# Hybrid decoder layer on one core: two products between gate sums and their splits, another load and split order ahead of the last projection, one weight sum moved

## Chip, core, metric

The kernel runs on one core of a Trainium2 chip. The metric is device time in microseconds of one execution. Engines: PE (TensorE, matmuls), DVE (VectorE), ACT (ScalarE), POOL (GpSimd), SP (SyncE, which issues nearly all transfers). Each engine works through its own instructions in order.

## The reference

One layer over 1024 tokens of width 1024, all in float32, cut to what matters here:

```python
proj = rmsnorm(x, norm_g) @ w_in                       # 9 kinds of columns
o_gla = gla_chunked(g_q, g_k, g_v, log_a)              # 4 heads, state carried over chunks
o_gla = rmsnorm(o_gla, gla_norm_g) * silu(g_gate)
y_a = o_gla @ w_pa
o_sb = stick_breaking(s_q, s_k, s_v) * silu(s_gate)    # 8 heads, causal, 128-query blocks
y_b = o_sb @ w_pb
gates = sigmoid(m_logits + b_gate)
x = x + (gates[0] * y_a + gates[1] * y_b) @ w_o
return rmsnorm(x, final_g)
```

## The kernel before

Every float32 operand is split into two float32r parts: ACT copies it to a high part, DVE subtracts that from the source for the low part (`split`, lines 167 to 169, and `o_hi`/`o_lo`, 1444 and 1448). A product then takes three matmuls per block of 128: high by high, high by low, low by high. The big projections use a Winograd form of a 2x2 block product: seven products of half-size operands instead of eight, on sums such as S1 to S4 (of the activations) and T1 to T4 (of the weights). A "product" below is 12 matmuls of 128x512.

- **Projection of w_in.** `pair_job` makes 31 jobs of seven products each, `Pairs` hands them out by units: `pairs.run(n)` does n products. In each job POOL makes T1 to T4 from the raw weights (lines 247 to 250), ACT and DVE split them. The first 25 products run beside the decay's exponentials (`djobs`), and beside `pjobs`: blocks j = 0 to 3 of w_pa are loaded, four sums each are made on DVE (`tp_sum`, 831), and the result is stored to `d_tp`, through one buffer. The next products up to `GLA_AT` = 63 run beside `tjobs`: the same for eight blocks of w_pb and w_o, into `d_t`.
- **GLA.** 32 steps (head h, block b of 128 tokens), with four products of the projection between the parts of each step. `gl_out` makes the block's output on PE and its norm: ACT sums squares, DVE scales, POOL takes the power (234), DVE multiplies (997). One step later `gl_gate` transposes it, multiplies it by the gate tile g (1007), splits and stores it. For b of 4 and more it then goes on at once: POOL makes four sums of g and of the gate tile gp four blocks back (1020), ACT and DVE split them, SP stores them to `d_os`. They are operands of the product with w_pa later. Tile g has four buffers, loaded by `gl_g`. ACT, DVE, PE, POOL and SP follow here the order that the tile scheduler gives them.
- **Stick-breaking attention.** 8 heads by 8 blocks: scores, sigmoid, a running product on DVE (1123), transposes and values; `values` multiplies by the gate (1161) and stores to `d_osb` (1163). Between them `Line` puts the products with w_pa (`pa_a`, `pa_b`, `pa_c`), listed by hand.
- **Transition.** The last eight products with w_pa, `pa_d`: for i = 0 to 3 first S3 by T3 (J = 1), then A22 by T4 into the same bank (J = 0). After each, `out_put` adds (1275), multiplies with the gate (1276) and stores. PE may go on in a bank only when DVE's addition has read it. Beside them the operands of the last projection (w_pb) are loaded from `d_osb` (A11, A12, A21, A22 by `a_load`, four 256 KB pieces each) and from w_pb and `d_t` (B11, B21, T2 and others by `o_load`), split, and summed on POOL (`sums`, 1406). From `manual.enter_context` on, the order on ACT, DVE and PE is the order of the code: all four splits of A11, two products, the splits of B11, two products, and so on.
- **Last projections.** 28 products with w_pb (`a_product`, four to each u), where `a_keep` and `a_merge` (the addition "kept", 1538) free the banks, then 28 with w_o, and the final norm.

## Time and profile before

| | |
|---|---|
| median of three runs | 1208.29 us (1207.48 to 1208.4) |
| the profiled execution | 1205.1 us |
| its span, first to last instruction | 1203.1 us |
| granted PE clock over the span | 0.992 |
| moved by DMA | 274.92 MB, 229 GB/s in the mean |

The span in 40 equal slices of 30 us, busy share in tenths, and the granted clock:

```profile
PE   8999999999999999999999999999999996899997
PEld 8998877887888788778888877888888885688886
DVE  6797776888677786776775776457888795978986
ACT  6556652333455555544444444235546353355543
POOL 1022221424243342542452252000000000900001
PEclk9999999999999999999999999999999997999999
```

Slices 0 to 9 are the projection up to GLA, 10 to 23 GLA, 24 and 25 the rest of the projection, 26 to 32 the attention, 33 and 34 the transition, the rest the last projections. A row of the timeline gives start, length, engine, line, operation, the tiles out<-in with their shape, and in brackets how long the engine had been idle before it and what ended the wait.

### The profile page before, as it was taken

How to read it: one execution, taken by the hardware profiler on the slowest of the kernel's cores; microseconds unless marked ns; L12 is line 12 of the kernel's file. 1: busy time of each engine (PE TensorE's matmuls, PEld its weight loads, DVE VectorE, ACT ScalarE, POOL GpSimd, SP SyncE). 2: the span in 40 equal slices, each digit the busy share in tenths (PEclk: the TensorE clock that was granted, in tenths of full speed). 3: DMA queues.
4: the chain of work that ended last, by engine and by line, in shares of the span. 5: the costliest groups of instructions: out<-in, count | busy, mean ns of one | idle time of the engine just before them, and what ended most of it. 6: DMA issues, size and time to landing. Idle time of an engine off the chain costs nothing.

```text
span 1203.1 us, 17066 instructions
## 1 busy us (share of the span) xinstructions
PE 1158.9 (96%) x5775; PEld 972.1 (81%) x5775; DVE 915.6 (76%) x1519; ACT 576.0 (48%) x1088; POOL 282.2 (23%) x281
## 2 busy tenths in 40 slices
PE   8999999999999999999999999999999996899997
PEld 8998877887888788778888877888888885688886
DVE  6797776888677786776775776457888795978986
ACT  6556652333455555544444444235546353355543
POOL 1022221424243342542452252000000000900001
PEclk9999999999999999999999999999999997999999
DMA  7326869997456765764655467889868879748652
GB/s 283 124 62 201 308 225 344 312 328 271 146 187 206 241 216 183 243 208 132 214 154 162 153 200 244 284 285 310 297 211 312 290 252 321 274 152 285 222 193 105
DMA packets 229299, 274.92 MB, mean 229 GB/s; under 512 B 14390, under 2 KB 165068, under 8 KB 226140
## 3 DMA queue, kind: packets, MB, share of 16 engines
q1 hardware_dynamic: 228636, 272.86, 68.6%
q8 instruction: 45, 0.74, 0.2%
q10 hardware_dynamic: 576, 0.98, 0.2%
q14 instruction: 42, 0.34, 0.1%
HBM read 168.93 MB, written 104.86 MB: 228 GB/s over the span
## 4 chain that ended last, share of the span: by engine, by line
PE 72%; issue 6%; DMA 6%; POOL 6%; DVE 6%; ACT 2%; SPq 1%; POOLq 0%; DVEq 0%; ACTq 0%
PE pp L273 12%; PE pp L274 12%; PE pp L275 12%; POOL g L1020 2%; PE pp L226 2%; PE pp L1254 1%; PE pp L1255 1%; PE pp L1256 1%; PE av L1156 1%; PE av L1158 1%; PE av L1157 1%; PE xa L1502 1%; PE xa L1501 1%; PE xa L1503 1%; PE xb L1625 1%
## 5 line engine op out<-in xcount | busy, mean ns | idle before, releaser
L273 PE MATMUL pp<-S,wh 128*128 128x512 f32 x372 | 147.4, 396 | 1.5 <-DVE f L555 1.5
L274 PE MATMUL pp<-S,wh 128*128 128x512 f32 x372 | 145.0, 390 | 0.0
L275 PE MATMUL pp<-S,wl 128*128 128x512 f32 x372 | 145.0, 390 | 0.0
L247 POOL TENSOR_TENSOR tt<-raw 128x512 f32<-128x512 f32 x31 | 43.4, 1400 | 267.9 <-DVE wl L169 256.4
L169 DVE TENSOR_TENSOR wl<-tt,wh 128x1024 fp32r<-128x1024 f32 x62 | 76.9, 1240 | 35.1 <-ACT wh L168 34.6
L312 DVE TENSOR_TENSOR f<-pp,f 128x512 f32<-128x512 f32 x93 | 63.7, 686 | 51.1 <-PE pp L275 46.4
L168 ACT ACTIVATE wh<-tt 128x1024 fp32r<-128x1024 f32 x62 | 65.6, 1057 | 63.0 <-PE pp L274 54.5
L1123 DVE TENSOR_TENSOR_SCAN be<-be,m 128x128 f32<-128x128 f32 (+3 forms) x64 | 86.2, 1349 | 4.9 <-ACT be L1120 4.9
L168 ACT ACTIVATE wh<-raw 128x1024 fp32r<-128x1024 f32 (+1 forms) x52 | 53.6, 1031 | 73.4 <-PE pp L274 31.3
L279 ACT ACTIVATE f<-pp 128x512 f32<-128x512 f32 x93 | 54.7, 590 | 65.2 <-PE pp L275 61.6
L169 DVE TENSOR_TENSOR wl<-raw,wh 128x1024 fp32r<-128x1024 f32 (+1 forms) x52 | 71.3, 1372 | 18.0 <-ACT wh L168 15.9
L273 PEld LDWEIGHTS pp<-S,wh 128*128 128x128 f32 x372 | 70.6, 190 | 16.6 <-ACT wh L168 1.9
L275 PEld LDWEIGHTS pp<-S,wl 128*128 128x128 f32 x372 | 69.9, 188 | 14.9
L274 PEld LDWEIGHTS pp<-S,wh 128*128 128x128 f32 x372 | 70.0, 188 | 13.7
L1120 ACT ACTIVATE be<-z 128x384 f32<-128x384 f32 (+4 forms) x96 | 47.0, 493 | 41.6 <-PE z L1119 35.6
L1406 POOL TENSOR_TENSOR N<-A,A 128x512 f32<-128x512 f32 x4 | 7.1, 1784 | 244.9 <-DMA A<-d_osb 244.9
L273 PE MATMUL pp<-ha22h,wh 128*128 128x512 f32 x124 | 49.4, 399 | 4.9 <-DVE f L312 4.9
L273 PE MATMUL pp<-S,dh 128*128 128x512 f32 x124 | 48.9, 394 | 3.7 <-ACT f L279 3.7
L234 POOL TENSOR_TENSOR r<-r,nhalf 128x1 f32<-128x1 f32 x40 | 24.0, 600 | 115.7 <-DVE r L233 114.4
L1020 POOL TENSOR_TENSOR g<-g 128x128 f32<-128x128 f32 x64 | 34.1, 532 | 71.4 <-DVE o L169 64.1
L273 PE MATMUL pp<-ha11h,wh 128*128 128x512 f32 x124 | 49.2, 397 | 0.0
L273 PE MATMUL pp<-ha12h,wh 128*128 128x512 f32 x124 | 49.0, 395 | 0.0
(556 smaller groups left out, 3504.1 us busy)
## 6 DMA issues: line engine op xcount, KB each, us to landing
raw<-in_w_in_dram SPq DMA_DIRECT2D x31, 1024.0 KB, 6.5
d_t<-t SPq DMA_DIRECT2D x16, 512.0 KB, 5.2
d_ogl<-o SPq DMA_DIRECT2D x64, 128.0 KB, 2.3
d_q<-o SPq DMA_DIRECT2D x16, 512.0 KB, 3.5
d_k<-o SPq DMA_DIRECT2D x16, 512.0 KB, 4.6
d_os<-o SPq DMA_DIRECT2D x32, 256.0 KB, 2.6
d_v<-o SPq DMA_DIRECT2D x32, 256.0 KB, 3.3
k<-d_k SPq DMA_DIRECT2D x8, 1024.0 KB, 6.1
```

The lines of the kernel that those rows point to most:

```text
L168: nc.scalar.activation(hi, src, AF.Copy)
L169: eng.tensor_sub(lo, src, hi.bitcast(F32))
L226: nc.tensor.matmul(pt[:, 0:n], *ops[kb][i], start=k == 0, stop=k == 3 * KB - 1)
L247: nc.gpsimd.tensor_sub(t1, b[:, 0, 1], b[:, 0, 0])
L273: nc.tensor.matmul(pt, bh[:, j], ah[:, j], start=first and j == 0, stop=False, skip_group_check=True)
L274: nc.tensor.matmul(pt, bh[:, j], al[:, j], start=False, stop=False, skip_group_check=True)
L275: nc.tensor.matmul(pt, bl[:, j], ah[:, j], start=False, stop=j == 3, skip_group_check=True)
L279: nc.scalar.activation(t[nm], t[bank], AF.Copy)
L312: nc.vector.tensor_add(add, bank, add)
L1020: nc.gpsimd.tensor_tensor(dst, x1, x2_, op=fn)
L1120: nc.scalar.activation(om[:, off + pc * w:off + (pc + 1) * w], zt[:, 0:w], AF.Sigmoid, scale=-inv_sqrt)
L1123: nc.vector.tensor_tensor_scan(rest, rest, m1[:, off:T][:, ::-1], 1.0, op0=ALU.mult, op1=ALU.max)
```

## The change

It has four parts, in the diff below.

1. GLA: the sums and their splits leave `gl_gate`. `gl_sum` (POOL) comes at the end of the step, `gl_sums_out` (splits and store) after two more products, ahead of `gl_g`; its place in ACT's and DVE's order is held.
2. The fourth block of w_pa (j = 3) moves from `pjobs` to `tjobs` as k = 8, the third block's later sums go from product 17 to 20, and `GLA_AT` is 67, so that GLA starts four products later.
3. Transition, loads: A11 ahead of the last weights (`wlast`), B21, the fourth pieces of A21 and A22 and T2 only after the last A load (`issue_after`), and pool `pq` on the other side. `pd_load(2)` moves into the attention's line, with two tiles of its own.
4. Transition, order of ACT and DVE: the splits of A11, B11 and A12 in halves between the additions of `pa_d`, which is called for one i at a time.

```diff
-GLA_AT = 63
+GLA_AT = 67
-    for j, (load_at, *sums_at, store_at) in enumerate(((0, 3, 4, 5), (6, 8, 10, 11), (12, 15, 17, 18), (19, 22, 23, 24))):
+    for j, (load_at, *sums_at, store_at) in enumerate(((0, 3, 4, 5), (6, 8, 10, 11), (12, 15, 20, 21))):
...
-    for k in range(8):
+    for k in range(9):
...
     def gl_gate(h, b):
-        t = gblk.pop((h, b))
+        t = gblk[h, b]
...
+    def gl_sum(h, b):
+        if b < 4:
             return
-        g, gp = t["g"], t["gp"]
+        g, gp = (gblk[h, b][nm] for nm in ("g", "gp"))
...
             nc.gpsimd.tensor_tensor(dst, x1, x2_, op=fn)
+    def gl_sums_out(h, b):
+        t = gblk.pop((h, b))
+        if b < 4:
+            return
         o = stage().rearrange("p e (s c) -> p e s c", c=P)
-        for i, src in enumerate((g, gp)):
-            split(src, *(o[:, e, 2 * i:2 * i + 2] for e in range(2)))
+        for i, nm in enumerate(("g", "gp")):
+            hi, lo = (o[:, e, 2 * i:2 * i + 2] for e in range(2))
+            tc.keep_in_program_order(nc.scalar.activation(hi, t[nm], AF.Copy))
+            tc.keep_in_program_order(nc.vector.tensor_sub(lo, t[nm], hi.bitcast(F32)))
...
         pairs.run(2)
+        if s > 1:
+            gl_sums_out(*steps[s - 2])
         gl_g(h, b)
         pairs.run(2)
         if s:
             gl_gate(*steps[s - 1])
         gl_out(h, b)
+        if s:
+            gl_sum(*steps[s - 1])
     pairs.run(3)
+    gl_sums_out(*steps[-2])
     gl_gate(*steps[-1])
+    gl_sum(*steps[-1])
+    pairs.run(2)
+    gl_sums_out(*steps[-1])
...
-    o_split("bA11", ALL)
-    st.run(1)
-    o_split("bB11", AB)
-    o_load("bB21")
-    a_load("A21", [3])
-    a_load("A22", [3])
+    o_split("bA11", (0, 1))
+    pa_d(0, 1)
+    o_split("bA11", (2, 3))
+    pa_d(1, 1)
+    wq_split("T4", 1, wlast)
+    pa_d(0, 0)
+    pd_load(3, (1,))[0]()
+    o_split("bB11", AB[:1])
+    pa_d(1, 0)
+    pd_load(3, (0,))[0]()
+    with tc.issue_after(last_a):
+        o_load("bB21")
+        a_load("A21", [3])
+        a_load("A22", [3])
+        o_load("bT2", "tt")
     sums("b", range(3), ("S1", "S3", "S2"), nc.gpsimd)
-    o_load("bT2", "tt")
+    pa_d(2, 1)
+    o_split("bB11", AB[1:])
```

SP's order at the transition before, from the last product's gate loads (`o<-d_ga`) to A11: `raw_10380` is B21, `tt_10401` T2, `d_osb7` the last store of the attention.

```order
L1306 DMA o_10367<-d_ga5_144 128x512
L1308 DMA o_10367<-d_ga4_143 128x512
L1422 DMA raw_10380<-in_w_pb_dram 128x4x128 x3
L1416 DMA tt_10401<-d_t0_165 128x512
L1416 DMA tt_10401<-d_t1_166 128x512
L1224 DMA wlast_10282<-d_tp_173 128x4x256
L1163 DMA d_osb7_115<-f_10237 128x512
L1396 DMA A11_10284<-d_osb0_108 128x512
L1396 DMA A11_10286<-d_osb2_110 128x512
L1396 DMA A11_10288<-d_osb4_112 128x512
L1396 DMA A11_10290<-d_osb6_114 128x512
```

And after the change, at the same place:

```order
L1333 DMA o_10211<-d_ga5_144 128x512
L1333 DMA o_10211<-d_ga4_143 128x512
L1413 DMA A11_10290<-d_osb0_108 128x512
L1413 DMA A11_10292<-d_osb2_110 128x512
L1185 DMA d_osb7_115<-f_10245 128x512
L1413 DMA A11_10294<-d_osb4_112 128x512
L1413 DMA A11_10296<-d_osb6_114 128x512
L1246 DMA wlast_10303<-d_tp_173 128x4x256
L1413 DMA A12_10305<-d_osb1_109 128x512
```

Two pieces of A11 now stand ahead of the attention's last store, the other two right behind it, and B21 and T2 follow the A loads further down.

DVE's order at the transition before, from the attention's last values (L1161) to the fourth pair of addition and multiplication of `pa_d`:

```order
L1161 SCALAR_TENSOR_TENSOR f_10237<-av_10239,vend_231,f_10237 128x128 x4
L1448 TENSOR_TENSOR bA11l_10320<-A11_10284,bA11h_10319 128x512
L1448 TENSOR_TENSOR bA11l_10320<-A11_10286,bA11h_10319 128x512
L1448 TENSOR_TENSOR bA11l_10320<-A11_10288,bA11h_10319 128x512
L1448 TENSOR_TENSOR bA11l_10320<-A11_10290,bA11h_10319 128x512
L1275 TENSOR_TENSOR f_10197<-pp_10329,f_10197 128x512
L1276 TENSOR_TENSOR f_10197<-f_10197,o_10196 128x512
L1275 TENSOR_TENSOR f_10204<-pp_10346,f_10204 128x512
L1276 TENSOR_TENSOR f_10204<-f_10204,o_10203 128x512
L169 TENSOR_TENSOR wl_10364<-wlast_10282,wh_10363 128x1024
L1448 TENSOR_TENSOR bB11l_10375<-raw_10292,bB11h_10374 128x1024 x2
L1275 TENSOR_TENSOR f_10198<-pp_10329,f_10198 128x512
```

And after it, from the same place:

```order
L1183 SCALAR_TENSOR_TENSOR f_10245<-av_10247,vend_231,f_10245 128x128 x4
L1466 TENSOR_TENSOR bA11l_10328<-A11_10290,bA11h_10327 128x512
L1466 TENSOR_TENSOR bA11l_10328<-A11_10292,bA11h_10327 128x512
L1297 TENSOR_TENSOR f_10198<-pp_10333,f_10198 128x512
L1298 TENSOR_TENSOR f_10198<-f_10198,o_10197 128x512
L1466 TENSOR_TENSOR bA11l_10328<-A11_10294,bA11h_10327 128x512
L1466 TENSOR_TENSOR bA11l_10328<-A11_10296,bA11h_10327 128x512
L1297 TENSOR_TENSOR f_10205<-pp_10354,f_10205 128x512
L1298 TENSOR_TENSOR f_10205<-f_10205,o_10204 128x512
L169 TENSOR_TENSOR wl_10372<-wlast_10303,wh_10371 128x1024
L1297 TENSOR_TENSOR f_10201<-pp_10333,f_10201 128x512
```

The first addition stands behind two splits instead of four, the second behind the other two, and the third no longer behind those of B11.

ACT's order in GLA before, in the step of head 0, block 6 (`o` from `g` are the splits of gate and sums, `wh` and `f` belong to the projection, `f` frees a bank):

```order
L168 ACTIVATE o_3966<-g_3766 128x256
L994 ACTIVATE on_3989,ssq_3990<-po_3982 128x256
L168 ACTIVATE knh_4019<-tr_4017 128x128
L168 ACTIVATE ash_4003<-am1_2693 128x128
L168 ACTIVATE o_3975<-g_3766 128x256
L168 ACTIVATE o_3975<-g_3768 128x256
L168 ACTIVATE wh_4038<-tt_3647 128x1024
L279 ACTIVATE f_4036<-pp_4023 128x512
```

And after it, for the same block (L1036 are the splits of the sums):

```order
L168 ACTIVATE o_4040<-g_3844 128x256
L168 ACTIVATE vh_4074<-vr_3928 128x256
L168 ACTIVATE knh_4086<-tr_4084 128x128
L168 ACTIVATE qsh_4232<-q2_3637 128x128
L168 ACTIVATE ash_4070<-am1_2771 128x128
L279 ACTIVATE f_4107<-pp_4094 128x512
L168 ACTIVATE wh_4143<-raw_3848 128x1024
L168 ACTIVATE o_4130<-f_4107 128x512
L1036 ACTIVATE o_4134<-g_3844 128x256
L1036 ACTIVATE o_4134<-g_3846 128x256
```

Before, the sums' splits follow the gate's within four instructions and stand ahead of `wh` and `f`; after, `f` and a weight split come between.

## The prediction

> **What bounds the kernel now.** I read the page's busy shares first, then its clock row and its chain, then every wait of TensorE (PE) in order of time, and for each long wait the other engines in the same microseconds.

> ```profile
> span 1203.1 us, 17066 instructions
> PE 1158.9 (96%) x5775; PEld 972.1 (81%) x5775; DVE 915.6 (76%) x1519; ACT 576.0 (48%) x1088; POOL 282.2 (23%) x281
> ...
> PE 72%; issue 6%; DMA 6%; POOL 6%; DVE 6%; ACT 2%; SPq 1%; POOLq 0%; DVEq 0%; ACTq 0%
> ```

> PE is busy for 96% and carries 72% of the chain, so an edit that leaves the matmuls alone can win only PE's idle time and slowed clock: 1203.1 - 1158.9 = 44.2 us, less what stays at both ends. The stretches say where it lies:

> ```profile
> 400.00:730.00 330.00, 321.53 (x1598) 262.85 (x1597) 242.66 (x524) 158.50 (x356) 126.29 (x139) 1.00 0.62 191
> 990.00:1045.00 55.00, 39.67 (x168) 31.96 (x167) 40.13 (x48) 19.32 (x29) 23.06 (x13) 0.84 0.83 285
> ```

> The columns are the stretch, its length, PE, PEld, DVE, ACT and POOL busy, the granted clock, DMA share and GB/s. In 990 to 1045 (last attention block, last four products with w_pa, first operands of the last projection) PE idles 15.3 us and the clock is 0.84; in 400 to 730 (GLA) it idles 8.5 us at full clock. These are the PE rows of the first place:

> ```profile
> 1006.70 0.39 PE L1256 MATMUL pp<-oa22h,wl 128*128 128x512 f32 x1
> 1018.16 0.79 PE L1254 MATMUL pp<-oa21h,wh 128*128 128x512 f32 x1 [11.08 <-DVE f L1275]
> 1022.87 0.40 PE L1256 MATMUL pp<-oa21h,wl 128*128 128x512 f32 x1
> 1035.71 0.47 PE L1254 MATMUL pp<-oa21h,wh 128*128 128x512 f32 x1 [4.25 <-DVE f L1275]
> 1040.13 0.39 PE L1254 MATMUL pp<-oa21h,wh 128*128 128x512 f32 x1
> 1061.89 0.39 PE L1501 MATMUL pp<-bA12h,bB21h 128*128 128x512 f32 x1
> 1062.12 0.39 PE L1502 MATMUL pp<-bA12l,bB21h 128*128 128x512 f32 x1
> ```

> At full clock matmuls of this shape start 0.23 us apart (the last two rows), so a product of 12 takes 2.75 us. From 1018.16 to 1022.87 eleven starts take 4.7 us instead of 2.5, from 1035.71 to 1040.13 twelve take 4.4 instead of 2.8. The two waits with their slow clock cost 11.1 + 2.2 + 4.25 + 1.6 = **19.2 us**. Both wait for the Vector (DVE) addition L1275, which frees the bank. Why that addition is late:

> ```profile
> 1005.06 1.13 DVE L1161 SCALAR_TENSOR_TENSOR f<-av,vend,f 128x128 f32<-128x128 f32 x4 [5.17 <-PE av L1158]
> 1014.87 2.64 DVE L1448 TENSOR_TENSOR bA11l<-A,bA11h 128x512 fp32r<-128x512 f32 x4 [8.68 <-ACT bA11h L1444]
> 1017.42 0.68 DVE L1275 TENSOR_TENSOR f<-pp,f 128x512 f32<-128x512 f32 x1
> 1014.20 2.58 ACT L1444 ACTIVATE bA11h<-A 128x512 fp32r<-128x512 f32 x4 [16.46 <-DMA A<-d_osb]
> 1001.78 0.33 SPq L1306 DMA_DIRECT2D o<-d_ga  x1
> 1002.62 2.13 SPq L1422 DMA_DIRECT2D raw<-in_w_pb_dram  x3
> 1006.56 0.56 SPq L1163 DMA_DIRECT2D d_osb<-f  x1
> 1007.16 10.66 SPq L1396 DMA_DIRECT2D A<-d_osb  x14
> ```

> The addition's own data lie ready; it stands behind four splits of A11, whose loads leave SP only from 1007.16.

> **The change, transition.** SP now puts A11's first two loads where the three raw loads began (1002.62), ahead of the store of 1006.56; its other two follow that store, and B21 and T2 come after all A loads. How long a 256 KB transfer takes here is bounded by two rows, and a load of that size just ahead lies between them:

> ```profile
> A<-d_osb SPq DMA_DIRECT2D x16, 256.0 KB, 5.4
> o<-d_ga SPq DMA_DIRECT2D x4, 256.0 KB, 4.1
> d_w<-f SPq DMA_DIRECT2D x1, 256.0 KB, 3.3
> ```

> I take 4.1, the nearest row (2.1 us of issue time for other loads is gone from ahead of it, but the line isn't empty). A11's second piece: issued 1003.1, landed 1007.2, ACT 0.65 (2.58/4), DVE 0.66 (2.64/4), the addition 0.68: PE resumes at 1009.2 and has waited 2.3 us since 1006.9. It then does one product to 1012.0. Its next bank needs the second addition, now behind pieces three and four: issued by 1007.7, landed 1011.8, through by 1013.8; a second wait of 1.8 us. Afterwards each addition stands in DVE's row before PE needs its bank: six products of 2.75 us are fed one by one, and the wait of 4.25 us, made by four splits ahead of the third pair of additions, is gone. PE then starts the last projection at 1027.5 and is at its eighth product, the one at 1061.89 now, by 1046.8.

> There DVE is late next. Its rows of now, with the GpSimd (POOL) sums beside them:

> ```profile
> 1021.78 1.95 POOL L1406 TENSOR_TENSOR N<-A,A 128x512 f32<-128x512 f32 x1 [244.95 <-DMA A<-d_osb]
> 1028.15 6.82 DVE L1448 TENSOR_TENSOR bA12l<-A,bA12h 128x512 fp32r<-128x512 f32 x4
> 1051.82 2.35 DVE L1448 TENSOR_TENSOR bT2l<-tt,bT2h 128x1024 fp32r<-128x1024 f32 x2
> 1056.65 0.69 DVE L1538 TENSOR_TENSOR kept<-pp,kept 128x512 f32<-128x512 f32 x1 [2.49 <-PE pp L1503]
> ```

> From 1014.87 to the end of bT2l at 1054.2 DVE has 39.3 us of work without a pause, and all of it still comes before the first addition "kept", which frees the bank of the eighth product. Now it may begin at 1006.2, when L1161 is done; it stands still 1.2 us for A11's first piece and 2.0 us for its third, and ends at 1006.2 + 39.3 + 3.2 = 1048.7; with the addition 1049.4. So PE reaches the eighth product at 1049.4 instead of 1061.9: **12.5 us** won, not 19.2. Bounds: with 3.3 us landings and no pause of DVE 15.7 (1046.2); with 5.4 us landings (2.6 us more over the two waits, at the price of a slowed clock of 1.6 if one of them passes 4 us) about 8. Behind that point the splits of S1, T1, S3 and T3 take DVE no longer than their products take PE, so I let the gain stand to the end.

> The Vector splits slow down beside POOL: four bA12l take 6.82 us, four bA11l alone 2.64. [...] The sum goes by the rows.

> **The change, GLA.** PE's waits in the GLA stretch, and what stands behind them:

> ```profile
> 409.29 0.50 PE L273 MATMUL pp<-S,dh 128*128 128x512 f32 x1 [2.19 <-ACT f L279]
> 500.35 0.50 PE L273 MATMUL pp<-S,dh 128*128 128x512 f32 x1 [1.49 <-ACT f L279]
> 527.32 0.50 PE L273 MATMUL pp<-ha22h,wh 128*128 128x512 f32 x1 [1.70 <-DVE f L312]
> 716.94 0.44 PE L1004 MATMUL tr<-ident,on 128*128 128x128 f32 x2 [0.94 <-DVE o L169]
> 725.51 0.63 PE L615 MATMUL tr<-ident,f 128*128 128x128 f32 x4 [1.48 <-DVE f L610]
> ...
> 407.39 0.42 ACT L168 ACTIVATE o<-g 128x256 fp32r<-128x256 f32 x1 [1.13 <-POOL g L1020]
> 407.71 1.04 ACT L168 ACTIVATE wh<-tt 128x1024 fp32r<-128x1024 f32 x1
> ...
> ACT o L168 <- POOL g L1020: 40.8, 29, 3.7
> ...
> L1020 POOL TENSOR_TENSOR g<-g 128x128 f32<-128x128 f32 x64 | 34.1, 532 | 71.4 <-DVE o L169 64.1
> ```

> Read backwards from 409.29: PE waits for ScalarE's (ACT) copy f, which came after the split wh at 407.71, which came after the split of the gate sum at 407.39, which waited for POOL. The other rows end in the same way. The five waits are 7.8 us. The change puts two products (5.5 us) and more between POOL's four sums (0.53 us each, with a power between them) and their splits, so these no longer stand still, and the copies of the projection no longer queue behind a POOL chain. What is late next is the power of the norm on POOL and the weight splits, both as before; and a start four products later shifts the partners. I leave one wait of 1.3 us: **6.5 us** won. Bounds: 7.8, and 3.0 if two waits like the largest now and one like 0.94 come at new places. The g loads now wait for sums two steps old; they are asked for one and a half steps (16 us) before use, and SP, on which they stand, has that much time.

> **The moved weight sum.**

> ```profile
> 161.99 0.50 PE L273 MATMUL pp<-ha22h,wh 128*128 128x512 f32 x1 [1.72 <-DVE f L312]
> 158.81 1.39 DVE L831 TENSOR_TENSOR tp<-tp 128x512 f32<-128x512 f32 x2
> 170.77 0.99 DVE L803 COPY ebl<-e 128x16 f32<-128x16 f32 x1 [2.92 <-ACT e L799]
> 190.98 0.47 PE L273 MATMUL pp<-S,wh 128*128 128x512 f32 x1 [1.50 <-DVE f L555]
> ```

> Two tp sums leave DVE at 158.81 and take **1.4 us** out of the wait at 161.99; three products later DVE idles (2.92 before 170.77) and hides them. The fourth block's four loads, four sums and store leave this stretch for one 30 products later. That may free the DMA line and end the wait at 190.98, or cost as much at the new place: between -1.5 and +1.5, and I take 0.

> **Sum.** 12.5 + 6.5 + 1.4 = 20.4 us. The profiled execution took 1205.1 us (span 1203.1, 2.0 around it), so it would take 1184.7; the three runs shown have a median of 1208.29, 3.2 above it, and there it is 1187.9: **1188 us**.

> **Rivals.**
> - *Vector binds the transition.* POOL's sums start some 5 us earlier and meet more of DVE's list, or the first loads take 5.4 us. For it: DVE has no pause in those 39.3 us now. Against it: POOL's work is no more than before. Gain 8 to 4 instead of 12.5, about 1195. [...]
> - *The GLA waits move instead of going.* All ACT and DVE rows there have other partners after a shift of four products. Gain 0 instead of 6.5: 1194. Against it: five of five waits end at POOL's gate sums.
> - *It doesn't do what it says.* A11 lands no sooner, since the DMA line and not SP's order set 1014.20: then the 19.2 stay and only 7.9 are won, 1200. Against it: four raw loads, two loads of T2 and the last weights leave the line ahead of it.
> - *Slower.* In GLA's 16 steps with sums, SP stands at the load of g until the splits two steps later have read the old tile, and weight loads queue behind it. It decides from a hold of 16 us, the lead of those loads; past it, each step would lose about what its waits are now, up to 2.2 us, and the price would be 35 us against 20.4: 1223.

> **Numbers.** Forecast 0.62, Vector 0.16, moved waits 0.11, no effect on the loads 0.05, slower 0.03, a cancelling mixture within 0.2% 0.03. The range takes in the bounds: best 15.7 + 7.8 + 2.9 = 26.4, 1182; worst 8 + 3 - 0.1 = 11, 1197. With a margin for the first two rivals it is 1181 to 1199, which leaves out the last three cases (0.11). About 0.2% (2.4 us) is what a measurement of this kernel can tell from no change. Faster 0.93, same 0.03, slower 0.04.

> **What would show it.** Right: PE's wait near 1006 is 1.5 to 3 us at full clock, a second of about 2 follows, one of 1 to 3 us stands at the eighth product of the projection, behind "kept"; ACT has nearly no wait for POOL's g, and the rows at 409, 500, 527, 717 and 725 are gone. Wrong: ACT's first bA11h starts after 1009 (counted from the same PE end), the clock in that stretch stays below 0.95, or PE waits of over 1 us appear in GLA behind other releasers.

## The result and the profile after

The median of five runs is 1188.7 us (1188.39 to 1191.52), beside 1208.29 us for the kernel before in the same series: a ratio of 0.9848, with a 95% interval of 0.9829 to 0.9866. The runs fall into two groups, three near 1188.5 us with a mean granted clock of 0.995 to 0.997, two at 1191.2 and 1191.5 with 0.993 and 0.994. The profiled one is the longest. The profile before lies 3.2 us below its median, this one 2.8 above: the spans differ by 13.6 us where the medians differ by 19.6.

From the page of the changed kernel, the span, the busy time and the granted clock (40 slices):

```profile
span 1189.5 us, 17064 instructions
...
PE 1160.4 (98%) x5775; PEld 972.5 (82%) x5775; DVE 916.9 (77%) x1519; ACT 577.1 (49%) x1088; POOL 278.3 (23%) x281
...
PEclk9999999999999999999999999999999999989999
```

PE is busy as long as before (1160.4 against 1158.9 us) in a shorter span: its pauses went, not its work. The two stretches of the prediction, same columns:

```profile
400.00:730.00 330.00, 327.61 (x1628) 268.60 (x1627) 246.58 (x540) 161.16 (x364) 124.01 (x143) 1.00 0.61 190
990.00:1045.00 55.00, 47.71 (x202) 38.34 (x202) 43.28 (x46) 22.68 (x34) 28.17 (x16) 0.95 0.87 295
```

In GLA PE idles 2.4 us instead of 8.5. ACT's waits for POOL's gate sums, 40.8 us in 29 waits before, are now (sum, number, longest):

```profile
ACT o L1036 <- POOL g L1026: 9.0, 6, 4.2
```

In 990 to 1045, which now reaches into the last projection, 7.3 instead of 15.3. PE's longest waits around GLA and in the transition, in order of time, with the matmuls behind them:

```profile
296.53 0.50 PE L273 MATMUL pp<-ha22h,wh 128*128 128x512 f32 x1 [2.30 <-DVE f L312]
429.72 0.50 PE L273 MATMUL pp<-ha22h,wh 128*128 128x512 f32 x1 [1.13 <-DVE f L312]
1001.29 0.50 PE L1276 MATMUL pp<-oa21h,wh 128*128 128x512 f32 x1 [2.30 <-DVE f L1297]
1002.38 0.63 PE L1276 MATMUL pp<-oa21h,wh 128*128 128x512 f32 x1
1002.81 0.63 PE L1277 MATMUL pp<-oa21l,wh 128*128 128x512 f32 x1
1043.93 0.80 PE L1531 MATMUL pp<-bA12h,bB21h 128*128 128x512 f32 x1 [4.99 <-DVE kept L1568]
1044.53 0.63 PE L1532 MATMUL pp<-bA12l,bB21h 128*128 128x512 f32 x1
1049.22 0.54 PE L1531 MATMUL xa<-bS2h,bT2h 128*128 128x512 f32 x1
```

The first wait of the transition is the 2.30 us that was forecast, but matmuls behind it start 0.43 us apart. The second transition wait of the prediction didn't come. The wait behind "kept" came with 4.99 us instead of some 2.6 (1049.4 - 1046.8), and the product behind it took 5.3 us (1043.93 to 1049.22) instead of 2.75.

What stood ahead of these waits on the other engines:

```profile
994.32 0.90 SPq L1413 DMA_DIRECT2D A<-d_osb  x2
998.67 1.19 ACT L1462 ACTIVATE bA11h<-A 128x512 fp32r<-128x512 f32 x2 [9.02 <-DMA A<-d_osb]
999.34 1.29 DVE L1466 TENSOR_TENSOR bA11l<-A,bA11h 128x512 fp32r<-128x512 f32 x2 [1.25 <-ACT bA11h L1462]
1002.76 1.30 DVE L1466 TENSOR_TENSOR bA11l<-A,bA11h 128x512 fp32r<-128x512 f32 x2 [0.73 <-ACT bA11h L1462]
1006.78 1.23 DVE L169 TENSOR_TENSOR wl<-wlast,wh 128x1024 fp32r<-128x1024 f32 x1 [1.33 <-ACT wh L168]
1027.21 6.19 POOL L1424 TENSOR_TENSOR A<-A,A 128x512 f32<-128x512 f32 x3
1038.53 0.63 ACT L1462 ACTIVATE bS2h<-A 128x512 fp32r<-128x512 f32 x1 [10.61 <-POOL A L1424]
1039.19 1.21 DVE L1466 TENSOR_TENSOR bS2l<-A,bS2h 128x512 fp32r<-128x512 f32 x1 [1.84 <-ACT bS2h L1462]
1043.19 0.68 DVE L1568 TENSOR_TENSOR kept<-pp,kept 128x512 f32<-128x512 f32 x1
```

A11's first loads now leave at 994.3 and are there for ACT at 998.7. Towards the end ACT stands 10.61 us for POOL: POOL made three S4 sums (6.19 us) before the sums of the fourth piece, whose S2 is needed first.

The ratio is that of all runs of a kernel to the kernel before in the same series (the medians of before lie between 1205.5 and 1208.3 us), and gains in us below are worked out from it. The stages are read from each kernel's one profile, by starts in the trace: the front (up to the last scores of the attention), from there to the first product S2 by T2 (transition and eight products), from there to the first product of w_o's T4. The rest is 18.4 to 18.8 us in all. PE's idle time in GLA is given where it is used; for the changed kernel it starts behind the wait at 296.53.

| kernel | ratio to before, 95% interval | front | scores to S2·T2 | S2·T2 to T4 | idle in GLA |
|---|---|---|---|---|---|
| before | 1 | 986.6 | 78.0 | 119.7 | 8.7 |
| changed | 0.9848 (0.9829 to 0.9866) | 978.5 | 70.7 | 121.7 | 3.2 |
| part 1 alone | 0.9917 (0.9901 to 0.9932) | 981.0 | 77.7 | 119.7 | 1.2 |
| part 2 alone | 1.0006 (0.9996 to 1.0016) | 989.9 | 79.0 | 119.7 | 11.0 |
| parts 3, 4 | 0.9944 (0.9932 to 0.9956) | 988.0 | 71.4 | 121.5 | 8.6 |
| part 3 alone | 0.9981 (0.9970 to 0.9992) | 988.7 | 73.9 | 121.5 | |
| part 4 alone | 0.9961 (0.9946 to 0.9976) | 987.3 | 71.7 | 120.2 | |
| parts 1, 3, 4 | 0.9868 (0.9851 to 0.9885) | 977.3 | 71.1 | 122.0 | |
| parts 1, 2, 4 | 0.9879 (0.9863 to 0.9896) | 977.6 | 72.3 | 121.3 | |
| changed, POOL's order | 0.9851 (0.9832 to 0.9869) | 975.2 | 69.6 | 121.9 | 2.5 |
| and T2 behind kept | 0.9835 (0.9819 to 0.9852) | 977.4 | 65.2 | 122.6 | |
| changed, 672 bytes | 0.9850 (0.9833 to 0.9866) | 979.1 | 69.5 | 119.7 | |
| all three | 0.9822 (0.9808 to 0.9837) | 978.1 | 65.4 | 120.9 | |

One thousandth is 1.2 us.

### The profile page after: what moved, and what is told of

The parts are those of the page before. It is cut to its first block, busy times and chain, and to the rows that moved or that the text cites. A ratio compares the mean times of both kernels' runs of the same rounds, so it can differ in the third digit from the quotient of the medians.

```text
span 1189.5 us, 17064 instructions
## 1 busy us (share of the span) xinstructions
PE 1160.4 (98%) x5775; PEld 972.5 (82%) x5775; DVE 916.9 (77%) x1519; ACT 577.1 (49%) x1088; POOL 278.3 (23%) x281
## 3 DMA queue, kind: packets, MB, share of 16 engines
q1 hardware_dynamic: 228780, 272.86, 69.6%
## 4 chain that ended last, share of the span: by engine, by line
PE 53%; DVE 5%; issue 2%; DMA 2%; SPq 1%; ACT 1%; POOL 1%; POOLq 0%; DVEq 0%; ACTq 0%
PE pp L273 8%; PE pp L274 8%; PE pp L275 8%; PE av L1178 1%; PE av L1180 1%; PE av L1179 1%; PE pp L1277 1%; PE pp L1278 1%; PE pp L1276 1%; PE tr L1157 1%; PE xb L1656 1%; PE xb L1655 1%; PE xb L1657 1%; PE z L1139 1%; PE z L1141 1%
## 5 line engine op out<-in xcount | busy, mean ns | idle before, releaser
L273 PE MATMUL pp<-S,wh 128*128 128x512 f32 x372 | 147.1, 395 | 0.0
L169 DVE TENSOR_TENSOR wl<-tt,wh 128x1024 fp32r<-128x1024 f32 x62 | 76.8, 1239 | 34.3 <-ACT wh L168 34.1
L312 DVE TENSOR_TENSOR f<-pp,f 128x512 f32<-128x512 f32 x93 | 63.8, 687 | 49.9 <-PE pp L275 46.0
L168 ACT ACTIVATE wh<-tt 128x1024 fp32r<-128x1024 f32 x62 | 65.5, 1057 | 61.4 <-PE pp L274 56.0
L168 ACT ACTIVATE wh<-raw 128x1024 fp32r<-128x1024 f32 (+1 forms) x52 | 53.7, 1033 | 72.4 <-PE pp L274 35.3
L279 ACT ACTIVATE f<-pp 128x512 f32<-128x512 f32 x93 | 55.0, 591 | 68.5 <-PE pp L275 64.2
L169 DVE TENSOR_TENSOR wl<-raw,wh 128x1024 fp32r<-128x1024 f32 (+1 forms) x52 | 70.0, 1345 | 17.9 <-ACT wh L168 17.3
L273 PEld LDWEIGHTS pp<-S,wh 128*128 128x128 f32 x372 | 70.5, 190 | 14.5 <-ACT f L279 0.4
L273 PE MATMUL pp<-ha22h,wh 128*128 128x512 f32 x124 | 49.3, 397 | 4.2 <-DVE f L312 4.1
L273 PE MATMUL pp<-ha11h,wh 128*128 128x512 f32 x124 | 49.2, 397 | 0.0
L273 PE MATMUL pp<-ha12h,wh 128*128 128x512 f32 x124 | 49.1, 396 | 0.0
L273 PE MATMUL pp<-S,dh 128*128 128x512 f32 x124 | 48.7, 393 | 0.0
L275 PE MATMUL pp<-ha11h,wl 128*128 128x512 f32 x124 | 48.4, 390 | 0.0
## 6 DMA issues: line engine op xcount, KB each, us to landing
d_os<-o SPq DMA_DIRECT2D x32, 256.0 KB, 3.0
d_v<-o SPq DMA_DIRECT2D x32, 256.0 KB, 3.5
```

What stands on the lines that cost most here:

```text
L168: nc.scalar.activation(hi, src, AF.Copy)
L169: eng.tensor_sub(lo, src, hi.bitcast(F32))
L273: nc.tensor.matmul(pt, bh[:, j], ah[:, j], start=first and j == 0, stop=False, skip_group_check=True)
L275: nc.tensor.matmul(pt, bl[:, j], ah[:, j], start=False, stop=j == 3, skip_group_check=True)
L279: nc.scalar.activation(t[nm], t[bank], AF.Copy)
L312: nc.vector.tensor_add(add, bank, add)
```

## Experiments

### Each part by itself

Theory: the terms of the prediction are separate, and each part brings its own. Rival in GLA: the start four products later (part 2) ended the waits, not the new place of the splits.

Part 1 alone:

```diff
     def gl_gate(h, b):
-        t = gblk.pop((h, b))
+        t = gblk[h, b]
...
+        if s > 1:
+            gl_sums_out(*steps[s - 2])
         gl_g(h, b)
```

> The kernel before with part 1 alone (sums and their splits two products later; GLA starts where it did). Theory: the new place of the splits ends the GLA waits, so PE's five rows of 0.94 to 2.19 us (7.8 us) go but for 1 to 2 us, and the time falls by 5 to 7 us, to about 1202; the waits of 1.72 and 1.50 us near 162 and 191 and the 15.3 us of the transition stay. Rival: the five waits went because GLA starts four products later and meets other partners; then part 1 alone leaves waits of 5 us or more in GLA and the time within 2 us of before.

Median 1197.84 us, ratio 0.9917: 10.0 us, more than expected. PE in GLA, before and then with part 1 alone (windows from the first to the last GLA step):

```profile
293.00:729.00 436.00, 427.33 (x2118) 349.63 (x2118) 320.12 (x685) 210.72 (x470) 162.99 (x175) 1.00 0.60 189
```

```profile
297.00:724.00 427.00, 425.84 (x2116) 349.56 (x2115) 321.33 (x683) 209.93 (x468) 161.68 (x175) 1.00 0.61 192
```

Idle time falls from 8.7 to 1.2 us, and the stage is 9 us shorter. Of the waits named only one of 0.94 is left. Part 1 delays the splits and also holds their place in ACT's and DVE's order; the two were not tried apart.

Part 2 alone:

```diff
-GLA_AT = 63
+GLA_AT = 67
...
-    for k in range(8):
+    for k in range(9):
```

> The kernel before with part 2 alone (fourth block of w_pa four jobs later, GLA four products later, sums still at once). Theory: 1.4 us of the wait near 162 go, and the wait of 1.50 us near 191 with it, while a new one of about 2 us stands at the start of GLA; the GLA waits of 0.9 to 2.2 us behind POOL's gate sums stay, at other places; the time falls by 0 to 3 us, to about 1207. Rival (the shift does it): the GLA waits fall below 3 us in all, and the time falls by 6 us or more, to 1202 or less.

Median 1207.21, ratio 1.0006: nothing. The wait at 162 shrinks from 1.72 to 0.70 us and the one at 191 goes, but GLA pays for it:

```profile
302.60:743.00 440.40, 429.39 (x2126) 350.22 (x2126) 321.18 (x689) 211.29 (x469) 162.21 (x177) 1.00 0.59 185
```

11.0 us idle instead of 8.7. So the shift did not end the GLA waits: the rival falls.

Parts 3 and 4 alone:

```diff
-    o_split("bA11", ALL)
-    st.run(1)
+    o_split("bA11", (0, 1))
+    pa_d(0, 1)
...
+    with tc.issue_after(last_a):
+        o_load("bB21")
```

> The kernel before with parts 3 and 4 alone (transition). Theory: the stretch from the last product S3 to the eighth product of the last projection is as in the changed kernel: a wait of 2.3 us, none of 4.25, one of about 5 us behind the addition kept, with slow clock behind it; gain 7 to 10 us, 1198 to 1201. If the prediction's own term held in undisturbed runs, 12.5 us, 1196. Rival: the gain of the transition depends on what the earlier parts do to the queues; then it is below 5 or above 14 us.

Median 1200.79, ratio 0.9944: 6.8 us, just below the expected 7 to 10, and far from 12.5. PE's waits there:

```profile
1011.47 0.80 PE L1254 MATMUL pp<-oa21h,wh 128*128 128x512 f32 x1 [2.92 <-DVE f L1275]
1027.42 0.50 PE L1254 MATMUL pp<-oa21h,wh 128*128 128x512 f32 x1 [0.56 <-DVE f L1275]
1054.55 0.79 PE L1509 MATMUL pp<-bA12h,bB21h 128*128 128x512 f32 x1 [4.94 <-DVE kept L1546]
```

The transition behaves as in the whole change, whatever the front does.

The whole without part 2 (the diff of part 2 undone):

```diff
-GLA_AT = 67
+GLA_AT = 63
...
-    for k in range(9):
+    for k in range(8):
```

> Parts 1, 3 and 4 without part 2 (weight sum and start of GLA as before). Theory: part 2, which is worth nothing alone, is worth 2 to 3 us beside part 1, because the waits of 1.7 and 1.5 to 2 us near 162 and 191 (with the clock that sometimes falls behind the second) are gone and part 1 takes away what a start four products later costs in GLA: 1190.5 to 1192. Rival: part 2 is worth nothing here either: 1188 to 1189.5.

Median 1190.64, ratio 0.9868 against 0.9848: 2.4 us, as the theory has it, but the intervals overlap, and the profiles do not show it: the front is 977.3 us without part 2 and 978.5 with it. The waits at 162 (2.01 us) and 191 (1.45) are back, but those at 296.53 (2.30) and 429.72 (1.13) are gone. So it is not shown that part 2 brings anything.

### Loads against order in the transition

Theory: PE's place at the eighth product is set by DVE's list, and that list by its first operand, so the loads bring most and the order by itself nothing. Rival: each wait counts by itself.

Part 3 alone, with the old order of the splits (the diff is against the changed kernel, its transition only):

```diff
-    o_split("bA11", (0, 1))
+    o_split("bA11", ALL)
     pa_d(0, 1)
-    o_split("bA11", (2, 3))
     pa_d(1, 1)
     wq_split("T4", 1, wlast)
...
+    o_split("bB11", AB)
```

> The kernel before with part 3 alone (A11 loaded sooner, B21 and T2 later, pool pq on the other side), the splits in the old order: four of A11 ahead of the first additions, four of A12 ahead of the third pair. Theory DVE (PE's place at the eighth product is set by when DVE can start its list): the waits of 11 and 4.2 us become about 6 and 4, no long wait behind kept, and the eighth product stands within 1.5 us of where both parts put it: 1200.5 to 1202.5. Rival (each wait of PE counts by itself): only the first shrinks, the second stays, and loads alone are worth 5 us and more less than both: 1205 or more.

Part 4 alone, with the old loads (against the kernel before):

```diff
-    o_split("bA11", ALL)
-    st.run(1)
+    o_split("bA11", (0, 1))
+    pa_d(0, 1)
+    o_split("bA11", (2, 3))
+    pa_d(1, 1)
```

> The kernel before with part 4 alone (splits of A11, B11, A12 in halves between the additions), loads in the old order. Theory DVE: PE's waits shrink to about 9.5 and below 2 us, but DVE's list starts no sooner, so that what is won comes back as a wait of 4 us or more behind kept at the eighth product: gain 0 to 2.5 us, 1205 to 1207.5. Rival (each wait of PE counts by itself): the 4.25 us and the slow clock behind it are won for good, gain 5 to 7 us, 1200 to 1202.

The loads alone: 1204.8 us, ratio 0.9981, 2.3 us. The order alone: 1201.42, ratio 0.9961, 4.7 us. Both miss what the theory expected and lie at the rival's numbers or next to them; their sum, 7.0 us, is about the 6.8 of both parts together. Before, kept was done at 1057.3 (1056.65 + 0.69) and PE came to its eighth product only at 1061.9: some 4.5 us could be won there with DVE starting no sooner, and the theory had left them out. With the loads alone both old waits remain, shorter:

```profile
1015.43 0.80 PE L1254 MATMUL pp<-oa21h,wh 128*128 128x512 f32 x1 [6.24 <-DVE f L1275]
1032.72 0.76 PE L1254 MATMUL pp<-oa21h,wh 128*128 128x512 f32 x1 [3.58 <-DVE pd L1275]
```

With the order alone the first wait is nearly the old one, and the second is nearly gone; kept runs without making PE wait:

```profile
1017.39 0.79 PE L1254 MATMUL pp<-oa21h,wh 128*128 128x512 f32 x1 [9.61 <-DVE f L1275]
1033.95 0.50 PE L1254 MATMUL pp<-oa21h,wh 128*128 128x512 f32 x1 [1.06 <-DVE f L1275]
1055.38 0.68 DVE L1542 TENSOR_TENSOR kept<-pp,kept 128x512 f32<-128x512 f32 x1
```

Counted from the last scores, kept starts at 68.1 us here and at 64.7 in the changed kernel (1043.19 - 978.5), while PE starts S2 by T2 at 71.7 and 70.7. So the earlier loads win 7.3 us at the first wait and bring kept 3.4 us sooner, but only 1.0 of that reaches the product behind: PE, now early, waits 4.99 us there and pays 2.5 us of slow clock for it.

Does part 3 then bring nothing? The whole without it:

```diff
-    wlast = wq_dma("T4", 1, mo.tile([P, KB, P], F32, tag="wr", name="wlast"))
...
+    pd_load(2)[0]()
     pa_d(0, 0)
...
-    with tc.issue_after(last_a):
-        o_load("bB21")
...
+    o_load("bB21")
```

> Parts 1, 2 and 4 without part 3 (A11 loaded late, operands of px where they were). Theory (what the earlier loads win at the first wait, about 7 us, is given back: 3 us more at kept, 2 us of slow clock behind it, 1.8 us by the place of px): the first wait is 9 to 10 us, none over 1 us at kept, and the time is 1187.5 to 1190. Rival (the earlier loads are what the transition gains): 1194 to 1196.

Median 1191.4, ratio 0.9879 against 0.9848: 3.7 us lost, between the theory's range and the rival's. Its two telling waits:

```profile
1008.36 0.80 PE L1276 MATMUL pp<-oa21h,wh 128*128 128x512 f32 x1 [10.28 <-DVE f L1297]
1062.29 0.50 PE L1529 MATMUL pp<-bS1h,bT1l 128*128 128x512 f32 x1 [0.90 <-DVE bT1l L1464]
```

Without the loads DVE is late once more behind kept: 121.3 us from S2·T2 to T4 where the old place of px (below) would allow 119.7. By the times part 3 is worth 2.1 us (6.8 - 4.7) to 3.7, a third to a half of what its first wait shows. The profiled spans, 1189.8 us without it and 1189.5 with it, do not show the 3.7, and the intervals behind that number just overlap.

### What sets kept

Theory POOL: the chain POOL's last S2, ACT's bS2h, DVE's bS2l and bT2l. Rival DVE: its list of splits.

```diff
-    sums("b", [3], ("S1", "S3", "S2"), nc.gpsimd)
+    s2_3 = sums("b", [3], ("S1", "S3", "S2"), nc.gpsimd)
...
-    sums("b", ALL, ("S4",), nc.gpsimd)
+    with tc.issue_after(s2_3):
+        sums("b", ALL, ("S4",), nc.gpsimd)
```

> The changed kernel, with POOL's three sums S1, S3, S2 of the fourth piece ahead of the four S4 sums. Theory POOL (the wait of 4.99 us behind kept is set by the chain POOL's last S2, ACT's bS2h, DVE's bS2l and two bT2l): ACT's wait of 10.6 us for POOL shrinks to about 4, DVE has no pause before the fourth bS2l, kept comes 2 us sooner, PE's wait is about 3 us and the slow clock of 2.4 us behind it shortens or goes: 1184 to 1187. Rival DVE (its own list of splits, slowed beside POOL, ends last): the wait stays 4.5 to 5 us and the time within 1 us of the changed kernel's 1188.7. If the two groups of times of the changed kernel (1188.5 and 1191.3) come from the clock behind that wait, this kernel has one group.

Median 1188.04 (1187.22 to 1193.03), ratio 0.9851: no change, and the times still lie 6 us apart. On DVE, ACT and PE:

```profile
1014.10 0.69 DVE L1297 TENSOR_TENSOR f<-pp,f 128x512 f32<-128x512 f32 x1 [3.26 <-DMA f<-d_w]
1030.02 0.63 ACT L1463 ACTIVATE bS2h<-A 128x512 fp32r<-128x512 f32 x1 [5.00 <-POOL A L1424]
1031.00 6.88 DVE L1467 TENSOR_TENSOR bS2l<-A,bS2h 128x512 fp32r<-128x512 f32 x4
1040.80 0.50 PE L1533 MATMUL pp<-bA12h,bB21h 128*128 128x512 f32 x1 [3.03 <-DVE kept L1570]
```

ACT's wait halves and DVE has no pause before bS2l. Yet kept starts 64.9 us behind the last scores (1040.07 - 975.2), as before (64.7): DVE had lost the time earlier, when a load of d_w came late, and its four bS2l run beside POOL for 6.88 us. PE's wait is shorter because PE comes later, 62.6 us behind the last scores instead of 60.5, after a second wait of 1.23 us at 1014.85. This points to the list as the bound, with POOL only its last pause. So the list was shortened ahead of kept:

```diff
+        if (u, i) == (1, 0):
+            for js in AB:
+                o_lo("bT2", js)
         nc.vector.tensor_mul(o[:, 0], bank, o[:, 0])
...
-            o_lo(nm, js)
+            if nm != "bT2":
+                o_lo(nm, js)
```

> The kernel with POOL's other order, and besides the two low splits of bT2 put on DVE behind the first addition kept. Theory DVE (its own list of splits sets kept, POOL's order does not): kept comes 2.35 us sooner, PE's wait at the eighth product falls from 3.0 to below 1 us, the clock stays at full speed behind it, and the time is 1184.5 to 1186 instead of 1188.0. Rival: the wait moves to the next product but one, S2 by T2, which then waits 2 us or more for bT2l or bS2l, and the time stays within 1 us of 1188.0.

Median 1186.74 (1185.8 to 1187.39), ratio 0.9835. The first kept, and PE's waits behind it and later:

```profile
1039.03 0.68 DVE L1570 TENSOR_TENSOR kept<-pp,kept 128x512 f32<-128x512 f32 x1
1039.76 0.50 PE L1533 MATMUL pp<-bA12h,bB21h 128*128 128x512 f32 x1 [0.71 <-DVE kept L1570]
1054.70 0.50 PE L1535 MATMUL pp<-bS1h,bT1l 128*128 128x512 f32 x1 [0.57 <-DVE bT1l L1467]
```

Kept starts 61.6 us behind the last scores (1039.03 - 977.4) instead of 64.9. PE waits 0.71 us instead of 3.03, at full clock, and S2·T2 starts after 65.2 us instead of 69.6. So the list sets kept, and S2·T2 does not wait: the rival falls. Some 0.6 to 0.9 us come back at S1 by T1, and the time falls by 1.3 us by the medians or 1.9 by the ratios, a little less than expected; the intervals overlap, so the trace shows this gain and the times do not.

### Where the operands lie

In the last projection of the changed kernel some products run slower at full clock. The tile view gives, for 16 matmuls of one kind, the shortest, median and longest duration in ns and the first and the last start:

```profile
L1655 PE MATMUL xb<-B11h,A11h x16: 394/395/395, 1104.2 to 1114.7; 128*128 128x512 f32 x16
...
L1655 PE MATMUL xb<-T2h,S2h x16: 389/390/397, 1126.6 to 1136.9; 128*128 128x512 f32 x16
```

Before, the first of them took 10.2 us (1119.0 to 1129.2), not 10.5; over a product's 48 matmuls the mean distance is 0.2334 us instead of 0.2267. The slow ones are A11·B11, A12·B21, S1·T1, S4·B22 and bS1·bT1: one operand in pool px, the other in hp or a21b. Products with both operands in px, or both in hp or a21b, lose under 1% (0.2267 to 0.2278 us). Pool pq moved to px's side, and px moved by pq's size, 4448 bytes by its tiles. By the compiled program's addresses, which no trace shows, px went from 256 to 416 modulo 512, and hp stayed at 256. Theory: the two operands' places matter. Rival: transfers or DVE beside them.

```diff
     fg = pq.tile([P, D], F32, tag="fg", name="fg", bufs=1)
+    pad = pq.tile([P, 168], F32, tag="pad", name="pad", bufs=1)
+    nc.gpsimd.memset(pad[:, 0:1], 0.0)
```

> The changed kernel with an unused tile of 672 bytes in pool pq, so that the operands in pool px begin where they did before modulo 1024 bytes (offset 256 modulo 512 again, as those of pool hp, instead of 416). Theory (place of the operands): the products A11 by B11, A12 by B21, S1 by T1, S4 by B22 and bS1 by bT1 start their matmuls 0.2267 us apart again instead of 0.2334, the stretch from the first bS1 product to the first wT4 product takes 108.8 us instead of 110.6, and the time falls by 1.8 us to about 1186.9. Rival (transfers or Vector beside these products slow them): the pitch stays 0.2334 and the time 1188.7.

```profile
L1657 PE MATMUL xb<-B11h,A11h x16: 389/389/389, 1102.9 to 1113.1; 128*128 128x512 f32 x16
```

10.2 us again, each of the five at 0.2267 or 0.2266, and 108.8 us from the first bS1 product to T4 instead of 110.6: shown in the trace. The time, 1188.31 (ratio 0.9850), does not show it; in this run the front was the longest of the changed kernels', and a difference of 1.8 us is the size of the spread of its runs. With 32 bytes instead, px at a multiple of 128:

```diff
+    pad = pq.tile([P, 8], F32, tag="pad", name="pad", bufs=1)
+    nc.gpsimd.memset(pad[:, 0:1], 0.0)
```

> The changed kernel with an unused tile of 32 bytes in pool pq: the operands of px begin 32 bytes lower, at a multiple of 128 bytes (384 modulo 512), those of hp stay at 256 modulo 512. Theory (they must begin at a multiple of 64 bytes): the products that started 0.2334 us apart start 0.2267 apart again. Rival (their places modulo 256 or 512 must agree): they stay at 0.233 or so. The time is not told apart by this.

The median of two runs is 1187.5 us. bS1·bT1 is at 0.233, the others at 0.232 to 0.233. So a multiple of 64 or 128 bytes isn't enough; whether 256, 512 or 1024 is the measure was not tried.

### All three together

```diff
+    pad = pq.tile([P, 168], F32, tag="pad", name="pad", bufs=1)
+    nc.gpsimd.memset(pad[:, 0:1], 0.0)
...
+    with tc.issue_after(s2_3):
...
+        if (u, i) == (1, 0):
+            for js in AB:
+                o_lo("bT2", js)
```

> The changed kernel with POOL's other order, the low splits of bT2 behind the first kept, and the 672 bytes that put the operands of px back in place. Theory: the two gains add, 2.0 us at kept with its clock and 1.8 us in the last projections: about 1185 against 1188.7 for the changed kernel and 1186.7 without the 672 bytes. Rival: what is won at kept is taken back by a wait of 1.5 us or more at the products S2 by T2 or S1 by T1, and the time stays at 1186.7 or above.

Median 1184.45 us (1183.69 to 1185.23), ratio 0.9822 (0.9808 to 0.9837), against 0.9848: 3.1 us better than the change, the fastest of all. Its runs lie within 1.6 us of each other. The interval overlaps that of the change, so the times make the 3.1 us likely and do not show them.

```profile
1040.61 0.50 PE L1535 MATMUL pp<-bA12h,bB21h 128*128 128x512 f32 x1 [0.75 <-DVE kept L1572]
1055.55 0.50 PE L1537 MATMUL pp<-bS1h,bT1l 128*128 128x512 f32 x1 [0.59 <-DVE bT1l L1469]
```

The wait behind kept is 0.75 us at full clock, and DVE is late next at bT1l.

## Why the prediction was right, and where it was not

The total was right (1188 forecast, 1188.7 measured), but two of its terms were off in opposite directions, and that it came within 0.7 us is luck. By the stages of the profiles the front gained 8.1 us (7.9 forecast), the transition 7.3 (12.5) and what follows lost 2.0 (nothing forecast): 13.6 us of span in all, with 0.2 in the rest. The medians, 19.6 us apart (18.4 by the ratio), add 6 us, since the profile before lies 3.2 us below its median and the one after 2.8 above.

- **GLA, forecast 6.5 us.** The mechanism was right: with the splits two products later the named waits went but for one of 0.94, ACT hardly stands behind POOL's gate sums any more (40.8 us in 29 waits before, 9.0 us in 6 in the changed kernel), and the rival of the shift fell. The size was too small: part 1 alone is worth 10.0 us. 7.5 of it is idle time, 1.0 more than the term, since the wait that was left is 0.94 and waits below 0.5 us went too. The rest is not in the profile of before: behind the wait of 2.19 us at 409 the clock stayed full there, but in three other profiles with the same GLA code (parts 3 and 4, part 3, part 4) it fell to half for 3.4 us behind the same wait, which costs 1.7 us. That this happens in most runs of the kernel before fits its median, 3.2 us above that profile, but was seen only in profiled runs. In the whole change GLA's idle time falls by 5.5 us (8.7 to 3.2), and a wait of 2.30 us, 0.55 before, stands just ahead of it.
- **The weight sum, forecast 1.4.** Alone it is worth nothing, since the later start makes GLA's old waits longer (11.0 us idle). Beside part 1 the 2.4 us of the ratios are not clear of noise, and the profiles do not show them. What it does at its new place was taken as 0, with bounds of 1.5 either way. Alone it was -2.1 by the ratio (-0.7 - 1.4), outside them; beside part 1 it stays open.
- **Transition, forecast 12.5.** Mis-sized: 6.8 us by time. ACT copied A11's first two pieces 4.4 us behind their issues at 994.3 and 994.8 (forecast 4.1), and the first wait was 2.30 us (2.3). DVE's list of 39.3 us was right too: between 998.1 and kept at 1043.2 lie 45.1 us, of which 5.6 are pauses. The step that failed is "it stands still 1.2 us for A11's first piece and 2.0 us for its third": the third piece cost 0.7, but the last weights 1.3 and POOL's S2 of the fourth piece 1.8 and 0.4 more through the copies of bT2, 2.4 us too many in all. That made the wait behind kept 4.99 us, and the clock fell to half for 6.83 us behind it: 2.5 us on the next product. 12.5 less 2.4 and 2.5 is 7.6; the trace has 78.0 - 70.7 = 7.3. That DVE's list sets PE's place there held: with the list shortened ahead of kept, PE's wait fell to 0.71 us. A further 2.0 us went where the prediction let the gain "stand to the end": part 3 moved pool px, and five kinds of products ran 3% slower (0.2334 us a matmul or a little more, instead of 0.2267).
- **Vector as the bound.** This rival (4 to 8 us) is what the transition did by itself, with another cause than the one weighed there. DVE's list came out 0.2 us longer than forecast (45.1 - 5.6 = 39.5 us against 39.3). DVE's splits bA12l ran 1.7 us each beside POOL as before (6.82 us for four before, 3.49 and 3.46 for two each after); before, the fourth bS2l, begun at 1051.2 when POOL's last sum had ended (1050.7), took 0.68 us against 1.78 of the slowest.
- **The statements to check.** Right: the waits near 409, 500, 527 and 725 gone, the loads sooner, a wait behind kept. Wrong: the size of that wait (4.99 us, not 1 to 3), the row at 717 gone (0.96 us at 707.96 is the same), full clock near 1006 (a half clock followed the 2.30 us), a second wait of about 2 us (the slowed product hid it), no wait over 1 us in GLA behind other releasers (one of 1.13 at 429.72 and one of 2.30 just ahead of it, both with part 2, neither with part 1 alone).

## What to carry to other kernels

When one part moves a wait, read what comes due next by its whole chain, also the engine that feeds the late one, and price the clock with the wait. Test the parts alone: a right total can stand on two wrong terms. When a pool moves, look at the mean distance of matmuls by operand before and after, not only at waits.

## What was not expected of the hardware

**Whether the clock falls behind a wait of about 2 us hangs on where the wait lies.** Over all 14 profiles, leaving out the first 15 us, PE's waits of 1.4 us and more, and whether the granted clock fell to half by three us behind them:

| PE waited | waits | clock fell |
|---|---|---|
| 1.40 to 1.79 us | 26 | 0 |
| 1.81 to 2.66 us | 18 | 7 |
| 2.89 to 11.08 us | 19 | 19 |

```profile
404.87:408.28 3.41, 2.23 (x10) 1.50 (x8) 1.69 (x6) 1.53 (x4) 2.33 (x5) 1.00 0.70 220
408.28:411.69 3.41, 2.40 (x11) 1.99 (x11) 2.59 (x5) 1.59 (x3) 0.00 (x0) 1.00 0.70 199
```

```profile
406.48:409.89 3.41, 1.22 (x6) 0.69 (x5) 2.50 (x6) 1.85 (x3) 1.05 (x2) 1.00 0.49 147
409.89:413.30 3.41, 3.41 (x10) 2.63 (x9) 1.66 (x3) 0.63 (x1) 0.00 (x0) 0.50 0.62 170
```

Before, the wait is split over two windows, PE is busy for 2.23 and 2.40 us of them, and the clock stays. With part 3 alone it lies in one window, PE is busy for 1.22 us of it, and the next window runs at half clock. Of the 4678 windows at full clock in the 14 profiles (again without the first 15 us), the clock fell behind all 24 in which PE idled for 55% or more and behind none of the 4651 with 51% or less; of three between, it fell behind two (53 and 55%). In the first 15 us, where PE's work is of other shapes, it fell behind three windows with about 45% (part 1 alone, part 2 alone, and all three together) and not behind two others.

The half clock lasted one window when PE was then busy (3.41 us from 1001.73 in the changed kernel), and each such window lost half of it, 1.7 us. Where the wait reached 0.6 us or more into the window at half clock, another followed (0.6 with parts 1, 3 and 4, behind kept); where it reached 0.5 us or less, none did (0.2 in the whole without part 3, behind the wait of 10.28). The wait of 4.99 us behind kept reached 1.2 us into it and had two, 6.83 us from 1042.69. That a wait lies otherwise in the grid from run to run would also explain why the runs of one kernel form groups about 3 us apart with different mean clocks; that last step is argued, not shown.

**An operand's place in a partition cost 3% of a product.** Where the moving and the stationary operand lay in different pools, and one pool was moved by 4448 bytes, a matmul of 128x512 started 0.2334 us behind the one before instead of 0.2267. Moved by 5120 bytes in all (4448 + 672), it was 0.2267 again; moved by 4480 (4448 + 32), 0.232 to 0.233. None of the profile's waits shows it.
